# Attention's value products: two key tiles together, one pair behind the scores

## The chip, the cores and the metric

The kernel runs on one core of a Trainium2 chip. The metric is the device time of one execution in microseconds (us), the median of several runs. The core's engines are TensorE (in the profile PE for the matrix products and PEld for the loads of their weights), VectorE (DVE), ScalarE (ACT), GpSimd (POOL) and SyncE (SP), which here issues the loads and stores. Each engine works through its own instructions in order, and semaphores make one wait for another.

## What is computed

Two blocks of a small sequence model, on 1024 tokens of 1024 features (and 16 prefixed tokens in the first block, 256 context tokens in the second). The change touches the attention in the last mixer of the second block: 8 heads, 1024 queries, 1280 keys (1024 of the sequence, 256 of the context), keys and queries of 96 features, values of 64.

```python
def _block_attention(q, k, v):
    ...
    scale = dk ** -0.5
    def one(qi):
        s = jnp.einsum('bqhd,bkhd->bhqk', qi, k, preferred_element_type=jnp.float32) * scale
        p = jax.nn.softmax(s, axis=-1).astype(v.dtype)
        return jnp.einsum('bhqk,bkhd->bqhd', p, v)
    ...
```

The attention's result is gated and goes with the other half of the mixer into a closing product and a layer norm (`_cd_out`, `_post_norm`).

## The kernel before

The program is one long unrolled list of instructions. The writer of the kernel calls engines in some order; a scheduler then orders each engine's instructions by their priority (the order in which they were written, unless told otherwise) and by a model of when their inputs are ready, gives out buffers of the pools, and sets the semaphores. So a line's place in the code is not its place on the engine.

Most matrix products multiply numbers split into two parts of a shorter format (float32r), in three products instead of one. The stages before the attention (first block, context path, Fourier mixer) take the first 2770 us of the profile. Then:

`prep(h)` makes ready head h's keys (L1500 to L1505: 6 products, copies on ScalarE, sums and splits on VectorE) and queries (L1508 to L1524: two blocks of 6 products L1516, a rotation and a split that go back and forth between ScalarE and VectorE). Then it takes the maximum of the scores from their leading parts: 24 products L1531 into the PSUM pool `psm` (4 banks, tag `sm`), each followed by a reduction on VectorE (L1532); the maxima are negated (L1536), transposed (L1538), and put as a row 96 into the queries through DRAM (L1540 to L1542), so that the score products subtract them.

`attend(h)` goes over the 1280 keys in KT = 10 tiles of 128. For a tile t and each half c of the queries (512 of them), three products L1555 make the scores in a bank of `pmm` (4 banks, tag `mm`), and ScalarE takes their exponential into `P` (L1556; 4 such tiles in the pool). Two products L1558 add the tile's share to the values' sum `po` (a bank of `psm`): the half c goes into the output partitions 64c to 64c + 63, so each uses 64 of the 128 columns of TensorE's array. They are in full float32, and each shows as two records in the trace. The softmax's sums are made by adding up the P tiles, even and odd ones in `sa0` and `sa1` (L1561, L1563; odd tiles of heads 0 to 5 on GpSimd, but for the last, the others on VectorE), and by four more products with ones behind the loop, L1573, the closing sums below: sa0 and sa1, for each half of the queries. Then come a reciprocal (L1575), the gate (L1569, L1576) and copies (L1582).

While head h is attended, `prep(h + 2)` runs beside it for h up to 5: the generator `nxt` is moved on by one step after each tile. Heads 6 and 7 have no such company; there the first inputs of the closing product are loaded and split (`split_in`, L74 to L76).

Of the kernel before, what the change touches and what calls it, by code (L numbers as in the profile page):

```python
# [11 lines left out]
AF = mybir.ActivationFunctionType  # L12
# [25 lines left out]
class Build:  # L38
# [20 lines left out]
    # ---- weights: raw -> exact split into two float32r parts  # L59
# [8 lines left out]
    # the sources side by side into the two parts of t  # L68
# [9 lines left out]
    # X: function (part, k, lo, hi) -> AP ; W: tile [128, 2, nk*128]  # L78
# [18 lines left out]
    # rsqrt(ps * scale + eps), one Newton step on top of the table's value  # L97
# [30 lines left out]
    # exp(x) in place on a small tile, x clamped to [-87, 88]  # L128
# [26 lines left out]
    # sin(th + shift) with the range brought to [-pi, pi]; shift 0 or pi/2  # L155
    def exact_sin(self, pool, out, th, shape, shift):
# [7 lines left out]
        if shift:  # L164
            # rounding of the sum above drops the quarter; redo it in two steps
            v.tensor_scalar(out=n, in0=th, scalar1=I2P, scalar2=0.25, op0=ALU.mult, op1=ALU.add)
            v.tensor_scalar(out=n, in0=n, scalar1=M, scalar2=None, op0=ALU.add)
# [14 lines left out]
    # ================= block 1 =================  # L182
# [20 lines left out]
    def block1(self, upto):  # L203
# [32 lines left out]
        # panel 1 (queries), 2 (values) of a head; 0: gates  # L236
# [13 lines left out]
    def z_panel(self, pool, tag, bufs=None):  # L250
        """the next product of the normed input that is wanted later only, kept in DRAM: queries and
        values of heads, tanh(x / 2) of the merge gates"""
# [17 lines left out]
    # panels chunk by chunk, where the chunks of X come one after the other  # L270
# [7 lines left out]
    def s5_params(self, pool, w1):  # L278
# [37 lines left out]
        # powers a^0..a^8, ascending (pa) and descending (pd)  # L316
# [18 lines left out]
        # bb = coef * b  # L335
# [10 lines left out]
        # scan multipliers [Ar|Ar], [-Ai|Ai]  # L346
# [7 lines left out]
    def cmul_tab(self, pool, pw, r0, r1, co, i):  # L354
        """out[128, 2, 4, 8, 16] = pw (over t) * co (over h) for the four pairs of panel i"""
# [15 lines left out]
    def s5(self):  # L371
# [5 lines left out]
        with ExitStack() as es:  # L377
# [17 lines left out]
            # first panels token chunk by token chunk, under the norm of the next chunk  # L395
# [3 lines left out]
            for c, (lo, hi) in enumerate(CH1):  # L399
                pss = [self.ps_mm()[:, 0:hi - lo] for _ in ws]  # L400
                # as the inputs of the first chunk come
# [19 lines left out]
            for i in range(8):  # L421
# [9 lines left out]
                # maps  # L431
# [28 lines left out]
                # chunk inputs to the states  # L460
# [7 lines left out]
            # outputs' factors, real and imaginary states on top of each other  # L468
# [6 lines left out]
            # scan over the chunks  # L475
# [9 lines left out]
            # outputs  # L485
            for i in range(8):
# [7 lines left out]
                # re(a^t c) over -im(a^t c)  # L494
# [24 lines left out]
    # ---- hgrn2  # L519
    def hgrn(self):  # L520
        nc, tc, A = self.nc, self.tc, self.A
        v = nc.vector
        with ExitStack() as es:
# [39 lines left out]
            for hd in range(8):  # L563
                # projections
# [28 lines left out]
                # decays inside the chunks of 16  # L593
# [16 lines left out]
                # queries and keys against the middle of their chunk of 32; QI: block, key chunk, query  # L610
# [3 lines left out]
                # meta chunk  # L614
# [8 lines left out]
                # chunk totals  # L623
# [9 lines left out]
                # queries decayed from the start of their chunk of 32, then from the middles of earlier chunks  # L633
# [7 lines left out]
                # products over the chunks of 16 before and after in the block of 128  # L641
# [14 lines left out]
                # queries against the carried state (in place of R)  # L656
                tt(out=R.rearrange("p (a s) -> p a s", s=32), in0=Qs.rearrange("p (a s) -> p a s", s=32), in1=pe2[:, :, 0].unsqueeze(2).to_broadcast([128, 32, 32]), op=ALU.mult)
                # keys into the state (in place of Bx)
                tt(out=B4[:, :, 0], in0=k4[:, :, 0], in1=B16(sx2, 0), op=ALU.mult)
                tt(out=B4[:, :, 1], in0=B4[:, :, 1], in1=B16(sx2, 1), op=ALU.mult)  # L660
                # token-major values and keys
# [16 lines left out]
                # states before each block  # L678
# [12 lines left out]
                # outputs  # L691
# [19 lines left out]
                # norm over the head's features, gate  # L711
                # (four token ranges side by side in the columns of the array, brought back by selections)
# [23 lines left out]
    # exact split of an fp32 tile into the two parts of t[:, :, lo:hi]  # L736
# [13 lines left out]
    # a product whose result goes on to a norm: the first panels panel by panel, the last nres  # L750
    # panels token chunk by token chunk, so that the norm of a chunk runs under the next chunk.
    # sq: the norm needs the sum of squares (else the plain sum) over all panels' rows r(i, lo, hi);
    # done(c, lo, hi, ps) gets that sum in every partition
# [43 lines left out]
    # sum over partitions of ns sources of n columns, in every partition: four sources at a time side  # L797
    # by side in the columns of the array, their sums brought together by a last product; the last
    # tail sources go into that one directly. tmp(): an [128, >= n] tile
# [22 lines left out]
    def merge(self):  # L822
# [5 lines left out]
        with ExitStack() as es:  # L828
# [50 lines left out]
            # h1 = h + (2 m) @ w_out / 2, then its norm  # L879
# [3 lines left out]
            # in place of the product's input, which a finished chunk no longer needs  # L883
# [109 lines left out]
    # ================= block 2 =================  # L993
    def mods(self, pool, cp):
        """shift, 1 + scale, gate / ALPHA of c (column 0) and c_ctx (column 1), features on partitions;
        the weights stream past the conditions, 128 inputs to 1024 features at a time"""
# [37 lines left out]
    # layer norm over features of a token chunk of x + gate / ALPHA * y, which is ALPHA * x + gate * y  # L1034
    # but for the scale: eps / ALPHA ** 2. r(k): AP of feature tile k, ps: its sum over features;
    # emit(k, d, rs): centred rows and 1 / deviation
    # sqt(k): tile for the squares of row k
# [15 lines left out]
    # LN(x) and the next mixer's input: n * g + b, n * g (1 + scale) + b (1 + scale) + shift  # L1053
# [16 lines left out]
    def ab_mixer(self, tp, yp, X, T, chunks, half_out, fill):  # L1070
        """pool heads then gating heads; half_out(which, tiles) takes the four feature tiles"""
# [86 lines left out]
    def ctx_path(self):  # L1158
        """the context through the first mixer and to the keys of the second"""
# [73 lines left out]
    # latent and rotary key rows of the second mixer, into DRAM at token base  # L1233
# [126 lines left out]
    def fourier(self, cp, tp, X):  # L1360
# [9 lines left out]
        # tokens on partitions, later in their place the spectra  # L1370
# [28 lines left out]
        # latents  # L1399
# [10 lines left out]
        # transform over tokens, then over features  # L1410
# [31 lines left out]
    def latents(self, tp, cq):  # L1442
        """normed latents, key weights"""
# [21 lines left out]
        # keys: both parts of the weights side by side in the columns  # L1465
# [7 lines left out]
    def mla(self, X):  # L1473
# [9 lines left out]
        with ExitStack() as es:  # L1483
            c0 = es.enter_context(self.pool("ml", side="right"))
            # key buffers: rows 0-63 the head's, 64-95 rotary, 96 ones against the row of -max
# [8 lines left out]
            def prep(h, tp):  # L1494
# [31 lines left out]
                # maximum of the scores, from their leading parts  # L1526
# [17 lines left out]
            def attend(h, nxt, tp):  # L1544
                """scores (keys on partitions), softmax weights, values"""
# [3 lines left out]
                P = {}  # L1549
                for t in range(KT):  # L1550
                    Pt = P[t] = tp.tile([128, 2, 512], F32, tag="P", name=self.nm("P"), bufs=4)
                    for c in range(2):
                        ps = self.ps_mm()
                        for i, (kp, qp) in enumerate(((0, 0), (0, 1), (1, 0))):
                            nc.tensor.matmul(ps, K[0:97, kp, 128 * t:128 * t + 128], Q[0:97, qp, 512 * c:512 * c + 512], start=i == 0, stop=i == 2)  # L1555
                        nc.scalar.activation(Pt[:, c], ps, AF.Exp, scale=scale)  # L1556
                    for c in range(2):
                        nc.tensor.matmul(po[64 * c:64 * c + 64, :], vv(t)[:, 64 * h:64 * h + 64], Pt[:, c], start=t == 0, stop=t == KT - 1)  # L1558
# [3 lines left out]
                    elif t > 3:  # L1562
                        eng.tensor_tensor(out=sa[t % 2], in0=sa[t % 2], in1=Pt, op=ALU.add)  # L1563
# [249 lines left out]
```

## Time and profile before

| | us |
|---|---|
| median of 3 runs | 3249.68 |
| lowest, highest run | 3247.68, 3250.23 |
| profiled execution: its span, first to last instruction | 3242.6 |
| of it, attention with the preparation of its first heads | 2770.0 to 3105.5 |
| before that | 0 to 2770.0 |
| closing product, layer norm | 3105.5 to 3242.6 |

For the profiled execution only the span is given, not a time taken from outside; it is 7.1 us below the median. All names of lines, L1558 and the like, are those of the kernel before; behind the change the lines of `attend` stand lower, and the sections that show its rows say which is which.

### The profile page before, as it was taken

The page shows a single profiled execution, that of the slowest core. Times are in us where ns is not written, and L with a number is a line of the kernel's source. Part 1 is how long each engine was busy: PE and PEld are TensorE (multiplying, and loading weights), DVE is VectorE, ACT ScalarE, POOL GpSimd, SP SyncE. Part 2 cuts the span into 40 slices and gives each one's busy share as a digit, 9 for nine tenths or more (in the row PEclk, how much of TensorE's full clock was granted, in tenths as well). Part 3 has the DMA queues.
Part 4 walks back from the last instruction along what each step waited for, and adds up shares of the span by engine and source line. Part 5 has one row for each costly group of instructions (what it writes and reads, how often), then busy time and mean ns, then how long its engine had stood idle before and what let it go on. Part 6 is the DMA issues. An engine that isn't in the chain of part 4 may idle for free.

```text
span 3242.6 us, 47786 instructions
## 1 busy us (share of the span) xinstructions
PE 3165.4 (98%) x19986; PEld 2840.8 (88%) x19986; DVE 1831.4 (56%) x3508; ACT 1126.1 (35%) x1846; POOL 92.9 (3%) x99
## 2 busy tenths in 40 slices
PE   8999899999999999999999999999999999999998
PEld 6999887879999999999999999989997889555476
DVE  7549468775454334465554555455336464777744
ACT  5341733233344312232222222252224353544532
POOL 0000000000210000000000000000000000121100
PEclk9999999999999999999999999999999999999999
DMA  4342454343552234111111111111111223000211
GB/s 153 90 161 91 148 182 142 118 153 103 158 155 81 91 118 130 33 59 46 40 46 53 47 52 40 53 35 54 46 40 66 92 88 130 29 7 7 79 49 52
DMA packets 106384, 269.01 MB, mean 83 GB/s; under 512 B 14798, under 2 KB 43694, under 8 KB 105974
## 3 DMA queue, kind: packets, MB, share of 16 engines
q1 hardware_dynamic: 99656, 245.35, 23.3%
q10 hardware_dynamic: 4464, 16.34, 1.3%
q0 software_dynamic: 2048, 4.26, 0.7%
q8 instruction: 157, 2.57, 0.3%
q14 instruction: 59, 0.48, 0.0%
HBM read 219.12 MB, written 46.11 MB: 82 GB/s over the span
## 4 chain that ended last, share of the span: by engine, by line
PE 90%; DVE 4%; DMA 2%; ACT 2%; issue 1%; SPq 0%; DVEq 0%; ACTq 0%
PE mm L83 62%; PE mm L949 7%; PE sm L1558 4%; PE mm L1555 4%; PE sm L813 2%; PE mm L1124 2%; PE sm L1531 1%; DMA YBd<-o 1%; PE mm L1516 1%; ACT Tt L502 1%; DVE R L604 1%; PE sm L465 1%; PE sm L1573 0%; PE sm L708 0%; PE sm L1017 0%
## 5 line engine op out<-in xcount | busy, mean ns | idle before, releaser
L83 PE MATMUL mm<-z,whl 128*128 128x256 f32 (+3 forms) x4032 | 682.9, 325 | 1.5 <-ACT z L231 1.0
L83 PE MATMUL mm<-a,whl 128*128 128x384 f32 (+1 forms) x4320 | 682.7, 319 | 1.6 <-ACT u L917 1.6
L83 PEld LDWEIGHTS mm<-a,whl 128*128 128x128 f32 x4320 | 678.5, 188 | 3.7 <-ACT u L917 1.9
L83 PEld LDWEIGHTS mm<-z,whl 128*128 128x128 f32 x4032 | 637.6, 189 | 36.8 <-issue 29.2
L76 DVE TENSOR_TENSOR whl<-wraw,whl 128x1024 fp32r<-128x1024 f32 (+2 forms) x258 | 302.6, 1178 | 221.1 <-ACT whl L75 220.3
L75 ACT CAST whl<-wraw 128x1024 fp32r<-128x1024 f32 (+2 forms) x258 | 260.6, 1014 | 341.8 <-PE mm L949 137.0
L83 PE MATMUL mm<-hx,whl 128*128 128x384 f32 (+1 forms) x2232 | 366.3, 322 | 7.7 <-ACT fx L1378 7.1
L83 PEld LDWEIGHTS mm<-hx,whl 128*128 128x128 f32 x2232 | 352.0, 189 | 16.8 <-ACT fx L1378 7.3
L949 PE MATMUL mm<-g,whl 128*128 128x384 f32 (+1 forms) x1584 | 257.9, 322 | 2.3 <-DVE f L951 1.2
L949 PEld LDWEIGHTS mm<-g,whl 128*128 128x128 f32 x1584 | 248.0, 188 | 13.9 <-issue 8.1
L83 PE MATMUL mm<-b,whl 128*128 128x384 f32 (+1 forms) x1152 | 180.9, 319 | 0.0
L83 PEld LDWEIGHTS mm<-b,whl 128*128 128x128 f32 x1152 | 180.8, 189 | 0.0
L917 ACT COPY u<-mm 128x384 f32<-128x384 f32 x132 | 58.3, 445 | 317.8 <-PE mm L83 317.8
L951 DVE TENSOR_TENSOR f<-f,mm 128x384 f32<-128x384 f32 (+1 forms) x240 | 118.3, 508 | 71.3 <-PE mm L949 70.4
L1556 ACT ACTIVATE P<-mm 128x512 f32<-128x512 f32 x160 | 94.7, 597 | 134.4 <-PE mm L1555 127.9
L83 PEld LDWEIGHTS mm<-y,whl 128*128 128x128 f32 x816 | 120.2, 188 | 13.1 <-issue 9.8
L83 PE MATMUL mm<-y,whl 128*128 128x256 f32 (+1 forms) x816 | 128.1, 312 | 1.4 <-ACT y L741 1.1
L1558 PE MATMUL sm<-P,m 128*64 128x512 f32 x320 | 128.0, 611 | 0.6 <-ACT P L1556 0.5
L1532 DVE TENSOR_REDUCE mx<-sm 128x1 f32<-128x512 f32 (+1 forms) x192 | 105.7, 595 | 39.7 <-PE sm L1531 38.4
L1555 PE MATMUL mm<-m,KB 97*128 97x512 f32 x420 | 121.7, 405 | 0.0
L1555 PEld LDWEIGHTS mm<-m,KB 97*128 97x128 f32 x420 | 75.6, 188 | 47.4 <-issue 33.3
L923 DVE TENSOR_SCALAR av<-u,conv_w,conv_b 128x1024 f32<-128x1024 f32 x22 | 17.9, 812 | 138.7 <-ACT u L917 138.7
(519 smaller groups left out, 3664.0 us busy)
## 6 DMA issues: line engine op xcount, KB each, us to landing
wraw<-w_up SPq DMA_DIRECT2D x44, 512.0 KB, 3.2
wraw<-w_h SPq DMA_DIRECT2D x32, 512.0 KB, 3.4
wraw<-ab_w SPq DMA_DIRECT2D x32, 512.0 KB, 3.4
wm<-ab_w_mod SPq DMA_DIRECT2D x24, 512.0 KB
wm<-cd_w_mod SPq DMA_DIRECT2D x24, 512.0 KB, 4.0
wraw<-w_down SPq DMA_DIRECT2D x22, 512.0 KB, 3.2
ut<-Ud SPq DMA_DIRECT2D x16, 520.0 KB, 4.5
gt<-Gd SPq DMA_DIRECT2D x16, 513.0 KB, 3.2
```

The lines of the kernel that those rows point to most:

```text
L75: self.nc.scalar.copy(t[:, 0], raw)
L76: self.nc.vector.tensor_tensor(out=t[:, 1], in0=raw, in1=t[:, 0].bitcast(F32), op=ALU.subtract)
L83: nc.tensor.matmul(ps, W[:, wp, wofs + 128 * k:wofs + 128 * k + 128], X(xp, kofs + k, lo, hi), start=first and k == 0 and i == 0, stop=las ...
L813: nc.tensor.matmul(p4[32 * j:32 * j + 32], self.ones[:, 0:32], x, start=i < 4, stop=i - len(pend) + j + 5 >= m)
L917: return u, (self.split_w(A["w_up"][p], [1024]), lambda c, lo, hi, ps: nc.scalar.copy(u[:, lo:hi], ps))
L949: nc.tensor.matmul(ps, ws[j][:, wp, 128 * o:128 * o + 128], G[j][:, xp, lo:hi], start=n_ == 0 and i == 0, stop=n_ == len(js) - 1 and i == 2)
L951: v.tensor_tensor(out=h1[o][:, 2 + lo:2 + hi], in0=h1[o][:, 2 + lo:2 + hi], in1=ps, op=ALU.add)
L1124: nc.tensor.matmul(ps, X(xp, k, 128 * t, 128 * t + 128), wv[k // 4][:, wp, 256 * (k % 4):256 * (k % 4) + 256], start=k == 0 and i == 0, st ...
L1532: v.tensor_reduce(out=mx[:, qt, j:j + 1], in_=ps, axis=mybir.AxisListType.X, op=ALU.max)
L1555: nc.tensor.matmul(ps, K[0:97, kp, 128 * t:128 * t + 128], Q[0:97, qp, 512 * c:512 * c + 512], start=i == 0, stop=i == 2)
L1556: nc.scalar.activation(Pt[:, c], ps, AF.Exp, scale=scale)
L1558: nc.tensor.matmul(po[64 * c:64 * c + 64, :], vv(t)[:, 64 * h:64 * h + 64], Pt[:, c], start=t == 0, stop=t == KT - 1)
```

## The change

`attend` no longer issues a tile's two value products right behind its exponentials. A function `values` issues the four of two tiles (t, c) = (a, 0), (a, 1), (b, 0), (b, 1); it is called after an odd tile for the two tiles of the pair before, and once behind the loop for the last pair. The products are written under a raised priority, and the first of the four gets an edge to the last exponential of the pair's second tile: the edge orders the scheduler and sets no semaphore (`NoSync`). The two calls that add up the P tiles stay where they were. Elsewhere the diff only takes comments out.

```diff
                 P = {}
+                def values(ts):
+
+                    with self.tc.high_priority():
+                        for t in ts:
+                            for c in range(2):
+                                mm = nc.tensor.matmul(po[64 * c:64 * c + 64, :], vv(t)[:, 64 * h:64 * h + 64], P[t][:, c], start=t == 0, stop=t == KT - 1)
+                                if t == ts[0] and c == 0:
+                                    self.tc.add_manual_dep(mm.ins, E[ts[1]].ins.name, mybir.DependencyInfo(
+                                        mybir.DependencyClass.NoSync, mybir.DependencyReason.DATA), reason="pair")
+
+                E = {}
+
                 for t in range(KT):
                     Pt = P[t] = tp.tile([128, 2, 512], F32, tag="P", name=self.nm("P"), bufs=4)
                     for c in range(2):
                         ps = self.ps_mm()
                         for i, (kp, qp) in enumerate(((0, 0), (0, 1), (1, 0))):
                             nc.tensor.matmul(ps, K[0:97, kp, 128 * t:128 * t + 128], Q[0:97, qp, 512 * c:512 * c + 512], start=i == 0, stop=i == 2)
-                        nc.scalar.activation(Pt[:, c], ps, AF.Exp, scale=scale)
-                    for c in range(2):
-                        nc.tensor.matmul(po[64 * c:64 * c + 64, :], vv(t)[:, 64 * h:64 * h + 64], Pt[:, c], start=t == 0, stop=t == KT - 1)
+                        E[t] = nc.scalar.activation(Pt[:, c], ps, AF.Exp, scale=scale)
...
                         eng.tensor_tensor(out=sa[t % 2], in0=sa[t % 2], in1=Pt, op=ALU.add)
+                    if t % 2 and t > 1:
+                        values((t - 3, t - 2))
                     next(nxt, None)
+                values((KT - 2, KT - 1))
```

How the rows move on TensorE is shown at three places. In the rows, mm and sm are banks of the two PSUM pools, P the exponentials, m_25199 to m_25201 the values of all heads, KB a head's keys, whl and cqn the query weights and their inputs, ones and sa the closing sums. Behind the change the value products are L1555 (before: L1558), the score products L1567 (before: L1555) and the closing sums L1586 (before: L1573).

First place: TensorE in head 1, from the values of tile 2 to the query products behind those of tile 3, beside the preparation of head 3's queries. Before:

```order
L1558 MATMUL sm_25687<-P_25732,m_25199 64x512 x2
L1500 MATMUL mm_25746<-ckn,wk 128x256 x2
L1555 MATMUL mm_25755<-m_25236,KB_25195 128x512 x3
L1555 MATMUL mm_25760<-m_25236,KB_25195 128x512 x3
L1516 MATMUL mm_25770<-cqn_23878,whl_24900 128x512
L1558 MATMUL sm_25687<-P_25754,m_25199 64x512 x2
L1516 MATMUL mm_25770<-cqn_23878,whl_24900 128x512 x2
L1516 MATMUL mm_25770<-cqn_23879,whl_24900 128x512 x3
```

With the change:

```order
L1567 MATMUL mm_25749<-m_25236,KB_25195 128x512 x3
L1567 MATMUL mm_25754<-m_25236,KB_25195 128x512 x3
L1516 MATMUL mm_25766<-cqn_23878,whl_24900 128x512
L1555 MATMUL sm_25687<-P_25728,m_25199 64x512 x2
L1555 MATMUL sm_25687<-P_25748,m_25199 64x512 x2
L1516 MATMUL mm_25766<-cqn_23878,whl_24900 128x512 x2
L1516 MATMUL mm_25766<-cqn_23879,whl_24900 128x512 x3
```

Tile 2's products, which stood ahead of tile 3's scores, have come down to stand in front of tile 3's; the place of the pair is the place that tile 3's had, one matmul behind its scores.

Second place: TensorE later in the same head, tiles 8 and 9 (P_25911 and P_25943 before, P_25907 and P_25937 with the change), among the products for the maxima of head 3. Before:

```order
L1558 MATMUL sm_25687<-P_25911,m_25201 64x512
L1555 MATMUL mm_25944<-m_25236,KB_25195 128x512
L1531 MATMUL sm_25902<-KB_24401,m_25768 128x512
L1555 MATMUL mm_25944<-m_25236,KB_25195 128x512 x2
L1555 MATMUL mm_25949<-m_25236,KB_25195 128x512 x3
L1555 MATMUL mm_25983<-m_25475,KB_25196 128x512
L1531 MATMUL sm_25905<-KB_24401,m_25768 128x512
L1558 MATMUL sm_25687<-P_25943,m_25201 64x512
L1531 MATMUL sm_25908<-KB_24401,m_25768 128x256
L1531 MATMUL sm_25925<-KB_24401,m_25768 128x512
L1558 MATMUL sm_25687<-P_25943,m_25201 64x512
```

With the change:

```order
L1567 MATMUL mm_25943<-m_25236,KB_25195 128x512 x2
L1531 MATMUL sm_25898<-KB_24401,m_25764 128x512
L1555 MATMUL sm_25687<-P_25907,m_25201 64x512 x2
L1555 MATMUL sm_25687<-P_25937,m_25201 64x512 x2
L1531 MATMUL sm_25901<-KB_24401,m_25764 128x512
L1531 MATMUL sm_25904<-KB_24401,m_25764 128x256
L1531 MATMUL sm_25919<-KB_24401,m_25764 128x512
L1567 MATMUL mm_25983<-m_25471,KB_25196 128x512 x3
```

The rows before begin with the second half of tile 8. The maxima's products that stood between the two halves of a tile now stand behind the pair, three in a row.

Third place: TensorE at the change from head 1 to head 2. Before:

```order
L1538 MATMUL sm_25959<-ident_99,nmx_25957 8x128
L1573 MATMUL sm_25969<-sa_25688,ones 64x512 x2
L1573 MATMUL sm_25969<-sa_25689,ones 64x512 x2
L1558 MATMUL sm_25979<-P_25982,m_25199 64x512 x2
L1558 MATMUL sm_25979<-P_26003,m_25199 64x512 x2
L1555 MATMUL mm_26030<-m_25475,KB_25196 128x512
```

With the change:

```order
L1538 MATMUL sm_25955<-ident_99,nmx_25953 8x128
L1586 MATMUL sm_25969<-sa_25688,ones 64x512
L1555 MATMUL sm_25979<-P_25982,m_25199 64x512 x2
L1555 MATMUL sm_25979<-P_26001,m_25199 64x512 x2
L1586 MATMUL sm_25969<-sa_25688,ones 64x512
L1586 MATMUL sm_25969<-sa_25689,ones 64x512 x2
L1500 MATMUL mm_26032<-ckn,wk 128x256 x2
```

The first pair of head 2 has moved in behind the first of head 1's four closing sums.

## Rows read from the trace of the kernel before

**Rows 1.** The page's first part: span, busy time by engine.

```profile
span 3242.6 us, 47786 instructions
...
PE 3165.4 (98%) x19986; PEld 2840.8 (88%) x19986; DVE 1831.4 (56%) x3508; ACT 1126.1 (35%) x1846; POOL 92.9 (3%) x99
```

**Rows 2.** Windows: stretch, length; busy time (instructions) by engine; clock, DMA share, GB/s.

```profile
2792.40:2830.70 38.30, 37.84 (x137) 18.90 (x138) 28.06 (x44) 17.77 (x33) 6.42 (x4) 1.00 0.00 1
2830.70:3047.20 216.50, 215.40 (x761) 110.94 (x759) 163.45 (x225) 102.25 (x178) 41.46 (x19) 1.00 0.04 12
2919.60:2962.00 42.40, 42.40 (x155) 22.08 (x153) 32.47 (x46) 19.84 (x35) 7.74 (x3) 1.00 0.02 7
3047.20:3105.50 58.30, 58.30 (x190) 24.23 (x186) 34.12 (x28) 33.49 (x49) 0.00 (x0) 1.00 0.36 126
```

**Rows 3.** The page's costliest groups: line, engine, operation, count; busy us, mean ns; idle.

```profile
L1558 PE MATMUL sm<-P,m 128*64 128x512 f32 x320 | 128.0, 611 | 0.6 <-ACT P L1556 0.5
```

**Rows 4.** Timeline of TensorE, blocks of value products: start, length, records.

```profile
2877.90 1.83 PE L1558 MATMUL sm<-P,m 128*64 128x512 f32 x4
...
2891.18 1.07 PE L1558 MATMUL sm<-P,m 128*64 128x512 f32 x2
...
3047.24 3.60 PE L1558 MATMUL sm<-P,m 128*64 128x512 f32 x16
...
3056.65 1.08 PE L1558 MATMUL sm<-P,m 128*64 128x512 f32 x4
```

**Rows 5.** Timeline of TensorE, 2880.0 to 2886.1 us, head 2.

```profile
2880.00 1.57 PE L1555 MATMUL mm<-m,KB 97*128 97x512 f32 x6
2881.40 0.40 PE L1516 MATMUL mm<-cqn,whl 128*128 128x512 f32 x1
2881.74 1.59 PE L1558 MATMUL sm<-P,m 128*64 128x512 f32 x4
2883.26 1.42 PE L1516 MATMUL mm<-cqn,whl 128*128 128x512 f32 x5
2884.51 1.56 PE L1555 MATMUL mm<-m,KB 97*128 97x512 f32 x6
```

**Rows 6.** Timeline, weight loads and ScalarE there; brackets: idle before, its releaser.

```profile
2881.73 0.19 PEld L1558 LDWEIGHTS sm<-P,m 128*64 128x64 f32 x2 [0.37 <-ACT P L1556]
2882.25 0.19 PEld L1558 LDWEIGHTS sm<-P,m 128*64 128x64 f32 x2 [0.33 <-ACT P L1556]
...
2880.90 1.30 ACT L1556 ACTIVATE P<-mm 128x512 f32<-128x512 f32 x2 [0.33 <-PE mm L1555]
```

**Rows 7.** Timeline of TensorE, the end of head 7.

```profile
3101.96 1.07 PE L1573 MATMUL sm<-sa,ones 128*64 128x512 f32 x2
3102.87 1.84 PE L1558 MATMUL sm<-P,m 128*64 128x512 f32 x4
```

**Rows 8.** Timeline of VectorE behind the closing sums, change from head 2 to 3.

```profile
2920.14 3.35 DVE L1575 RECIPROCAL rz<-sm 128x512 f32<-128x512 f32 x1
...
2923.96 0.67 DVE L1576 TENSOR_TENSOR gt<-gt,rz 128x512 f32<-128x512 f32 x1
...
2925.15 0.41 DVE L1503 TENSOR_TENSOR kt<-kt,mm 64x256 f32<-64x256 f32 x1
2926.57 1.19 DVE L1505 TENSOR_TENSOR KB<-kt,KB 64x256 fp32r<-64x256 f32 x1 [1.01 <-ACT KB L1504]
2927.79 0.69 DVE L1520 TENSOR_TENSOR qu<-mm,ropet 64x512 f32<-64x512 f32 x1
2929.11 1.23 DVE L1563 TENSOR_TENSOR sa<-sa,P 128x1024 f32<-128x1024 f32 x1 [0.63 <-ACT P L1556]
2930.37 0.68 DVE L1522 TENSOR_TENSOR qt<-qt,qu 32x512 f32<-32x512 f32 x1
```

**Rows 9.** Waits in heads 0 to 7, and reductions' busy time in head 2919.6:2962.0.

```profile
PEld sm L1531 <- DVE mx L1532: 16.1, 19, 1.4
...
2919.60:2962.00 42.40, 13.31 (x24) 1.00 0.02 7
```

## The prediction

> **What bounds the kernel now.** I read the page's first part first [rows 1]: TensorE is busy for 98% of the span and its granted clock is 1.00 in every window below, so time can only go where TensorE's own stream gets shorter, or come where it stops. Next I read the windows of the attention stage [rows 2]: head 0, heads 1 to 5, one of those alone, heads 6 and 7. TensorE is busy practically all the time in each, while VectorE has 163.45 of 216.50 us in heads 1 to 5 and ScalarE 102.25. A busy TensorE is not a full one, though, and the third view shows it: the products of the values (L1558) alone take 128.0 us, for 160 products in 320 records (two records make one product) [rows 3].
>
> The timeline tells why that is dear. One product standing alone, a block of 2 records, takes 1.07 us [rows 4]. Where both query halves of a tile are ready, the block of 4 records takes 1.08 us: the halves write different 64 output columns and go side by side, so the second costs nothing. But mostly a tile's block of 4 takes 1.59 or 1.83 us [rows 4, 5]. The weight loads say what for: the second half's load at 2882.25 ends a wait of 0.33 us for ScalarE's exponential [rows 6]. Two exponentials take 1.30 us in a row, from 2880.90 to 2882.20 [rows 6], and the score products that feed the later one had ended about 2881.4: the values stand directly behind their own scores, so half c=0 starts and half c=1 comes 0.52 to 0.76 us later. Eight halves that need not wait (16 records, 4 tiles) take 3.60 us [rows 4], that is 0.43 us more for each half-step of both columns: (3.60 - 1.08) / 6 = 0.42.
>
> Counted through the timeline from 2792.4 to 3104.5, start to start (which leaves out the 0.07 us by which a block's last record overlaps the next one), the 80 tiles stand in 91 blocks: 48 single products of 1.00 (24 tiles), 14 blocks of 1.76, 16 of about 1.52, 4 of 1.02, 9 blocks joined to others or to the closing sums (22 tiles, 19.8 us). Together 120.9 us; 128.0 less 91 tails of 0.08 gives the same.
>
> **The change, part by part.** *Values in pairs.* In the new order all four products of two tiles stand together, in all 40 pairs. A pair alone takes one tile's 1.01 and two further steps of 0.43: 1.87 us. 29 pairs stand alone, 54.2 us; 11 stand next to another pair or to the closing sums, where four steps of 0.43 suffice, 19.1 us. Sum 73.3 instead of 120.9: **48 us less**. The exponentials should be there: between the last score product of the pair's second tile and the pair there are one to three matmuls, and the first tile's two steps take another 0.9 us, so the half that waited until 0.85 us behind its scores (2881.4 to 2882.25) is asked for only 1.2 us behind them.
>
> *Fewer changes of kind.* Entering a block of values costs TensorE something besides: the L1516 matmul before the block takes 0.34 us to the block's start, where six L1555 take 1.40, 0.233 each; the five behind it take 1.25 to 2884.51 instead of 1.17 [rows 5]. I take 0.19 a block. 91 blocks become 38 (4 in head 0, 5 in each of heads 1 to 5 and 7, 4 in head 6): 53 x 0.19 = **10 us less**.
>
> *The closing sums.* Before, the four sums of a head (L1573) stand together, and 8 records take 1.94 us, after which the next head's values follow. Now, at six changes of head, the first pair of the next head has slipped in behind the first sum. That sum holds column half 0; the first value product wants the same half and stands ahead of the one for half 1. In the one place of the trace with this order, the sum's two records start at 3101.96 and the value product of half 0 only at 3102.87 [rows 7]; half 1 starts later still, but it also waited for its exponential, so the row leaves open whether it would have gone ahead. Either four steps of 0.86 remain (0) or there are five (0.86 a head). I take the dear end, since nothing in the trace starts ahead of an earlier product that waits: 6 x 0.86 = **5 us more**. The Trainium skill, TensorE: Matmul & The Clock Gate, Part 3: Packing small matmuls, says that matmuls start in program order; by it the 5 us stand, without it they would be 0.
>
> TensorE's sum: 48 + 10 - 5 = 53 us less. By head: 6 in head 0, 3.6 in head 6, 8 in head 7, which leaves about 35 for heads 1 to 5, or 43.3 to 36 us a head.
>
> *What is late next.* VectorE is busy 32.47 us in a head of 42.40 [rows 2]; in one of 36 it has 3.5 to spare. Two places can fail. First, the chain behind the closing sums. The reciprocal (3.35) starts when they end; behind it come the gate product (0.67, its step 0.6), the last key piece (0.41 and 1.19), the query rotation (0.69 and 0.68) [rows 8], between them three ScalarE steps of about 0.6 and two exponentials ahead of the last of them. Before the head's first maximum product (L1531) can start, that is about 3.3 + 0.4 + 0.6 + 1.2 + 0.7 + 0.6 + 0.7, and 1.8 for the exponentials and the copy: 9.3 us. In the new order TensorE has between the same two points two short matmuls, 30 of 0.234, and one pair with its entry: 0.24 + 7.0 + 2.06 = 9.3. So the cover is just used up. Second, the maxima: three products now come in a burst behind each pair, with three score banks to take them, and the reductions that free these banks already kept weight loads waiting 19 times, 16.1 us, most of it covered [rows 9]. This new cost is not in the trace; it lies between 0 (cover holds) and the 4 to 5 us a head at which VectorE would keep half of its present idle time. I take 1 us a head for six heads, nearer to 0 because VectorE's own work of the maxima part, 24 reductions in 13.3 us [rows 9] and two additions of 1.23, fits into the 19 us that TensorE has there, and 2 us at the very end, where the last pair has no later scores to cover its exponential and the last addition (1.23). **8 us more.**
>
> *At nothing* I cost: ScalarE (some 20 of 36 us a head), GpSimd's additions (7.74 us a head, far from the end), the loads for the closing product (the DMA engines are 36% busy in the last window, [rows 2]; if they came late, the time lost would be theirs, a few us at most), and the held P tiles: there are four, the pair reads the older two before the next tile's scores are done.
>
> Sum: 53 - 8 = 45 us. The profile's span is 3242.6 us, 7.1 under the median of the runs, 3249.7; the rest lies around the span and isn't touched. So 3249.7 - 45 = **3205 us**.
>
> **The rivals.** *All of it.* If the sums don't cost a fifth step and VectorE stays covered, 58 - 1 = 57 us go: 3193. For it: VectorE has 3.5 us a head over. Against: the chain that just fits.
>
> *VectorE sets the pace.* It then keeps its present waits of 8 to 9 us a head beside its 32.47, some 41 us a head: heads 1 to 5 give 216.5 - 205 = 11.5, the others 15.6: 27 us, **3223**. For it: reductions and products hang on three banks, and today's weight loads already wait for them. Against: those waits are mostly for TensorE itself. The Trainium skill, TensorEngine Tiling (Array Packing), PSUM Bottleneck, warns of just this: side-by-side products speed up TensorE but not the reading of PSUM, which may become the bottleneck. No trace here shows it yet.
>
> *Nothing side by side.* If the second half's delay were not the exponential but something fixed, blocks would take 1.5 to 1.8 a tile as now and only the 10 us for changes remain, less the 5: 3245, within what I call the same. The block of 1.08 and the 3.60 for four tiles [rows 4] speak against it.
>
> *Slower.* ScalarE takes its work in order, and in the new order its copies that wait for VectorE (the gate, the rotated queries) stand ahead of tile 4's exponentials, which the third pair needs. If the 9.3 us chain stood uncovered in front of that pair at each of six heads, 6 x 9.3 = 56 us would be added to a gain of 53, with 5 to 10 for what queues behind: 3255 to 3260. It decides from 8.8 us a head. Against it: thirty matmuls and a pair cover it.
>
> **How the numbers follow.** Forecast 0.60, all of it 0.15, VectorE's pace 0.17, nothing side by side 0.04, slower 0.04. The first three are faster by more than 0.2% (6.5 us, about what a measurement of this kernel can tell from no change): 0.92; same 0.04; slower 0.04. The forecast's own range is 3198 to 3215 (5 us for the sums, 10 for VectorE); with the neighbours on both sides, 3191 to 3225.
>
> **What would show it.** The values' busy time should fall from 128.0 to about 76 us, in blocks of 8 records of 1.94; weight loads of values waiting for the exponential should nearly vanish; heads 1 to 5 should last 36 to 38 us, with VectorE near 90% and its waits for maximum products shorter; the closing sum's records should show one step of half 0 alone. Blocks of 8 that still take 3 us, or heads of 41 us with weight loads waiting for reductions, would prove me wrong.

## The result and the profile after

The changed kernel takes 3194.30 us (median of 4 runs, 3191.73 to 3194.65), the kernel before beside it 3248.68 (4 runs, 3244.17 to 3250.23): a ratio of 0.9839, 95% interval 0.9825 to 0.9852, or 54.4 us less. The forecast was 3205 with a range of 3191 to 3225: right in sign and inside the range, 11 us too careful.

Behind the change the value products are L1555, the scores L1567, the exponentials L1568, the additions of the P tiles L1571 and L1573, the closing sums L1586, the reciprocal L1588 and the gate products L1582 and L1589. The preparation keeps its lines.

The page's first part answers to [rows 1]: VectorE and ScalarE do what they did, TensorE is busy 56 us less.

```profile
span 3192.9 us, 47786 instructions
PE 3109.1 (97%) x19986; PEld 2838.8 (89%) x19986; DVE 1830.5 (57%) x3508; ACT 1121.4 (35%) x1846; POOL 93.1 (3%) x99
```

The windows answer to [rows 2]. They run from one L1538 to the next, which is where the preparation of a head ends: head 0, head 1, heads 2 to 5, one of those alone, heads 6 and 7. Columns as there.

```profile
2794.12:2824.13 30.01, 29.12 (x126) 17.52 (x125) 26.72 (x42) 15.62 (x29) 5.48 (x3) 1.00 0.00 1
2824.13:2864.99 40.86, 37.92 (x155) 22.99 (x154) 34.70 (x46) 19.98 (x37) 11.02 (x6) 0.96 0.03 7
2864.99:3008.23 143.24, 142.16 (x607) 86.06 (x606) 128.41 (x181) 80.17 (x145) 31.64 (x14) 1.00 0.05 16
2936.37:2972.10 35.73, 35.42 (x152) 21.39 (x151) 31.83 (x46) 19.28 (x36) 7.48 (x3) 1.00 0.02 8
3008.23:3056.62 48.39, 47.81 (x202) 24.84 (x201) 35.74 (x30) 32.67 (x52) 0.00 (x0) 1.00 0.43 152
```

A steady head went from 42.40 to 35.73 us, with TensorE still busy all but 0.3 of it and VectorE now at 31.83 of 35.73, 89%. One head stands out: head 1, 40.86 us, with 2.9 us in which TensorE does nothing and a mean granted clock of 0.96. Between the same instructions of the kernel before, head 0 took 36.50, heads 1 to 5 216.56 and heads 6 and 7 (to the last closing sum) 62.1; now 30.01, 184.10 and 48.39. That is 52.7 us less. Of it the span shows 49.7, since the stages ahead of the attention took 1.9 and those behind it 1.1 us longer in this execution.

TensorE's timeline at the change from head 3 to head 4 and behind it answers to [rows 4, 5, 7]. Records of two lines that overlap are listed apart.

```profile
2936.37 0.28 PE L1538 MATMUL sm<-ident,nmx 128*8 128x128 f32 x1
2936.57 0.64 PE L1586 MATMUL sm<-sa,ones 128*64 128x512 f32 x1
2936.59 0.64 PE L1555 MATMUL sm<-P,m 128*64 128x512 f32 x1
2937.05 0.59 PE L1586 MATMUL sm<-sa,ones 128*64 128x512 f32 x1
2937.07 1.87 PE L1555 MATMUL sm<-P,m 128*64 128x512 f32 x6
2938.40 0.59 PE L1586 MATMUL sm<-sa,ones 128*64 128x512 f32 x1
2938.77 0.59 PE L1555 MATMUL sm<-P,m 128*64 128x512 f32 x1
2938.82 1.45 PE L1586 MATMUL sm<-sa,ones 128*64 128x512 f32 x5
2940.21 0.50 PE L1500 MATMUL mm<-ckn,wk 128*128 128x256 f32 x2
...
2942.27 1.94 PE L1555 MATMUL sm<-P,m 128*64 128x512 f32 x8
2944.14 1.42 PE L1516 MATMUL mm<-cqn,whl 128*128 128x512 f32 x5
```

The pair at 2942.27 is as forecast: 8 records in 1.94 us, 1.87 to the next start; all 29 lone pairs of the attention are like it. The place above it was forecast wrongly. In program order the first closing sum, for half 0, is followed by the pair's products for half 0, half 1, half 0, half 1, and then by the other sums. The first sum (2936.57) holds column half 0; the first value product wants that half too and must wait. Yet a value product starts 0.02 us behind the sum (2936.59), so it can only be the next in order, the one for half 1. From 2936.57 to 2940.21 the four sums and the pair take 3.64 us: four steps, not five.

Three of the waits from 2794 to 3057 us (us in total, times, longest):

```profile
PEld sm L1531 <- DVE mx L1532: 15.1, 24, 2.4
PEld sm L1555 <- ACT P L1568: 8.0, 28, 0.3
PE sm L1531 <- DVE mx L1532: 3.3, 5, 1.9
```

The value products' loads waited 31.7 us in 79 places for exponentials before, now 8.0 in 28, none over 0.3. The loads of the maxima wait for reductions much as they did [rows 9].

### The profile page after: what moved, and what is told of

It reads as the page before. It is cut to its first block, busy times and chain, and to the rows that moved or that the text cites. A ratio compares the mean times of both kernels' runs of the same rounds, so it can differ in the third digit from the quotient of the medians.

```text
span 3192.9 us, 47786 instructions
## 1 busy us (share of the span) xinstructions
PE 3109.1 (97%) x19986; PEld 2838.8 (89%) x19986; DVE 1830.5 (57%) x3508; ACT 1121.4 (35%) x1846; POOL 93.1 (3%) x99
## 4 chain that ended last, share of the span: by engine, by line
PE 87%; DVE 6%; ACT 3%; DMA 3%; issue 1%; SPq 0%; DVEq 0%; ACTq 0%
PE mm L83 63%; PE mm L949 7%; PE mm L1567 3%; PE sm L813 2%; PE sm L1555 2%; PE mm L1124 2%; DMA YBd<-o 1%; PE sm L1531 1%; ACT Tt L502 1%; DVE R L604 1%; PE sm L465 1%; DMA wm<-ab_w_mod 0%; PE sm L708 0%; PE sm L1017 0%; PE sm L687 0%
## 5 line engine op out<-in xcount | busy, mean ns | idle before, releaser
L1567 PE MATMUL mm<-m,KB 97*128 97x512 f32 x420 | 118.2, 401 | 1.3 <-ACT P L1568 1.3
L1568 ACT ACTIVATE P<-mm 128x512 f32<-128x512 f32 x160 | 91.5, 596 | 68.6 <-PE mm L1567 50.9
L1567 PEld LDWEIGHTS mm<-m,KB 97*128 97x128 f32 x420 | 76.9, 191 | 24.9 <-issue 7.3
L923 DVE TENSOR_SCALAR ag<-u,conv_w,conv_b 128x1024 f32<-128x1024 f32 x22 | 17.9, 813 | 119.1 <-ACT u L917 119.1
```

Source lines behind the costliest of these rows:

```text
L1568: E[t] = nc.scalar.activation(Pt[:, c], ps, AF.Exp, scale=scale)
```

## The experiments

Times of runs are medians; each ratio is against the kernel before on the same chip, and the changed kernel's is 0.9839. The stages ahead end at 2764 us in one profiled execution and at 2770 in another, so I also compare "the attention", from the start of the first L1538 to the start of the last record of the closing sums: 343.6 us before, 291.0 changed. "Blocks" are TensorE's unbroken stretches of value products and closing sums, from a block's start to the start of what follows: 92 with 137.0 us before, 38 with 88.5 changed.

**e_onecol: nothing side by side.**

```diff
-mm = nc.tensor.matmul(po[64 * c:64 * c + 64, :], vv(t)..., P[t][:, c], start=t == 0, stop=t == KT - 1)
+o = po[64 * c:64 * c + 64, :] if t == 0 else po[0:64, :]
+mm = nc.tensor.matmul(o, vv(t)..., P[t][:, c], start=t == 0, stop=c == 1 if t == 0 else t == KT - 1 and c == 1)
```

> The changed kernel, where the values' products of half 1 go into the output partitions of half 0 from the second tile on, so that no two of them can go side by side: the sums of the values of both halves run together and the attention's output is another; count and size of the instructions stay. Theory (side by side is what makes the second half free): 0.86 us more for each of 9 tiles in 8 heads, 62 us: 3256, a lone pair 3.6 us instead of 1.87. Rival (products of the two halves do not overlap much; the gain came from waits and fewer blocks): 3194 to 3215.

Measured: 3255.69 us, ratio 1.0030 (1.0019 to 1.0041). A lone pair:

```profile
2884.55 3.65 PE L1556 MATMUL sm<-P,m 128*64 128x512 f32 x8
2888.13 1.44 PE L1516 MATMUL mm<-cqn,whl 128*128 128x512 f32 x5
```

3.58 us to the next start instead of 1.87; blocks 149.8 us, 61 more than changed, and the time 61 more. The theory's 62 stands: the column halves are worth more than the whole gain.

**e_single and e_behind: one tile at a time.** In e_single `values((t - 1,))` is called after each tile (and for the last one behind the loop), with the edge to that tile's own last exponential, `E[ts[-1]]`.

```diff
-if t % 2 and t > 1:
-    values((t - 3, t - 2))
+if t:
+    values((t - 1,))
```

> The changed kernel, but with the values of one key tile at a time, one tile behind the scores, under the same priority and edge. TensorE's order then has 66 blocks of value products and closing sums, 55 of them one tile standing alone, where the changed kernel has 38 (29 lone pairs) and the kernel before 92. Theory (what pays is that both query halves of a tile are ready and go side by side; an entry into a block costs about 0.19 us): 55 lone tiles at 1.01 us and 25 joined ones at 0.86 give 77 us instead of 73, and 28 more entries cost 5: about 9 us more than the changed kernel's 3194, so 3203. Rival (what pays is the number of blocks: 54 us for 54 blocks, 1 us each): 28 us more, 3222.

Measured: 3226.66 us, 0.9942 (0.9929 to 0.9954). By number that is the rival, but the trace says why it didn't test it. The edge put each block right behind its own exponential, so the second half was late again, as before the change (the row is for 2794 to 3060 us; to the end of the attention it is 28.9 us in 77 waits):

```profile
PEld sm L1555 <- ACT P L1568: 25.2, 66, 0.9
```

```profile
2923.70 1.90 PE L1555 MATMUL sm<-P,m 128*64 128x512 f32 x4
2925.53 1.44 PE L1567 MATMUL mm<-m,KB 97*128 97x512 f32 x5
```

I had moved two things at once. The 55 lone tiles took 1.49 us on average, not 1.01. Against e_single, e_behind moves the edge alone, to the next tile's exponential (the diff is against the changed kernel; the calls are those of e_single):

```diff
-... E[ts[1]].ins.name, ...
+... E[min(t + 1, KT - 1)].ins.name, ...
```

> The changed kernel with one tile's value products at a time, each block put behind the last exponential of the next tile, so that both its halves have long been ready. (In the run e_single the block stood right behind its own tile's exponentials, and its loads still waited for them 66 times, 25.2 us; it did not tell the entries' price.) TensorE's order has 64 blocks, 47 of them one lone tile, instead of 38 with 29 lone pairs. Theory (waiting for the exponential was the cost; an entry costs 0.19): lone blocks of 1.01, together 76 us instead of 73, 26 entries more at 0.19 cost 5: 8 us more than the changed kernel, 3202, and the loads' wait for exponentials stays near nothing. Rival (it is the number of blocks that costs, 1 us each, as e_single's 32 us for 28 blocks would also have it): 26 us more, 3220.

Measured: 3199.40 us, 0.9855 (0.9838 to 0.9871).

```profile
2904.76 1.08 PE L1555 MATMUL sm<-P,m 128*64 128x512 f32 x4
2905.77 1.43 PE L1516 MATMUL mm<-cqn,whl 128*128 128x512 f32 x5
```

All 47 lone tiles take 1.01, the wait for exponentials is 2.3 us, and 64 blocks cost hardly more than 38: 36.47 us a steady head instead of 35.73. Of these 0.74 the blocks' own steps make 0.45, which leaves 0.1 for each of three more entries. So one tile at a time, with both halves ready, already has some nine tenths of the gain (28 of the 54 blocks fewer are part of that); pairing brings the rest.

**e_noedge: priority alone.** The three lines of the edge are taken out.

> The changed kernel without the edge, the raised priority kept. TensorE's order falls apart again: 90 blocks, 49 of them a single half of a tile, as good as the 92 with 48 single halves of the kernel before. Theory (only the order counts, and the edge makes it): 3240 to 3250, the single halves 1.00 us each. Rival (the priority brings the values forward and with that most of the gain): below 3215.

Measured: 3244.33 us, 0.9989 (0.9980 to 0.9998); blocks 131.8 us, 49 single halves of 1.00, loads waiting 25.9 us for exponentials in the attention (before: 31.7). As expected, the edge makes the order; priority without it brings 4 us.

**e_crossed: how far a product may overtake.**

```diff
-for t in ts:
-    for c in range(2):
+for c in range(2):
+    for t in ts:
```

> The changed kernel with each pair's four products in another order: tile a half 0, tile b half 0, tile a half 1, tile b half 1. Nothing else moves. Theory (each half of the columns has a queue of its own, so a product for a free half starts ahead of an earlier one that waits for the other half, as the closing sums of the changed kernel show): no change, 3194 within 3, blocks of 8 records of 1.94. Rival (matmuls start in program order, as the prediction took it for the closing sums): in each pair the second half-0 product holds up half 1 by 0.86 us; 40 pairs, 34 us, 3228.

Measured: 3202.94 us, 0.9871 (0.9855 to 0.9886): neither number, and the trace shows both theories at work in different places. The change from head 3 to head 4 and the first lone pair behind it:

```profile
2939.81 1.07 PE L1586 MATMUL sm<-sa,ones 128*64 128x512 f32 x2
2940.72 1.94 PE L1555 MATMUL sm<-P,m 128*64 128x512 f32 x8
2942.43 1.94 PE L1586 MATMUL sm<-sa,ones 128*64 128x512 f32 x6
2944.30 0.50 PE L1500 MATMUL mm<-ckn,wk 128*128 128x256 f32 x2
...
2946.36 1.94 PE L1555 MATMUL sm<-P,m 128*64 128x512 f32 x8
```

In the lone pair a half-1 product stands behind one waiting half-0 product and overtakes it: 1.87 us, as in 21 of the 29 lone pairs. In seven others half 1 began 0.13 to 0.48 us behind half 0, and one ran at a granted clock of 0.67 (1.99 to 2.77 us). At the change of head it stands behind two waiting ones and does not: the sum runs alone for 0.91 us and the block takes 4.49 instead of 3.64. Five such places and one of 6.21 instead of 5.35 make 5.2 us, the eight slower pairs 2.8; the attention is 7.2 us longer.

**e_quad4: groups of four.**

```diff
-if t % 2 and t > 1:
-    values((t - 3, t - 2))
+if t in (3, 7):
+    values(range(t - 3, t + 1))
...
-... E[ts[1]].ins.name, ...
+... E[ts[-1]].ins.name, ...
```

> The changed kernel with groups of four, four and two tiles instead of five pairs, still with four P tiles: 29 blocks of values and closing sums instead of 38. Theory (TensorE sets the time; a lone block costs 0.15 us beyond its steps of 0.43 and 0.19 for the entry): 9 blocks fewer, 3 us less: 3191. Rival (ScalarE: the exponentials of the fifth tile can't start until the group has read the first, and nothing feeds VectorE for 3.6 us, which at 90% cannot catch up): 1 to 2 us more a head, 3200 to 3210.

Measured: 3200.91 us, 0.9860 (0.9846 to 0.9875). By number this is the rival: 37.2 us a steady head, 1.5 more. TensorE stops there for 1.6 us a head, the longest stop just ahead of the second group (the bracket: idle before, its releaser):

```profile
2918.73 0.50 PE L1531 MATMUL sm<-KB,m 96*128 96x512 f32 x1 [1.19 <-DVE mx L1532]
2919.51 3.65 PE L1555 MATMUL sm<-P,m 128*64 128x512 f32 x16
```

TensorE waits there for VectorE's reductions, not for ScalarE's exponentials. But what made VectorE late just ahead of the stop is an addition on GpSimd, the matter of the next runs:

```profile
2915.85 2.10 DVE L1522 TENSOR_TENSOR qt<-qt,qu 32x512 f32<-32x512 f32 x1
```

```profile
2915.01 2.39 POOL L1573 TENSOR_TENSOR sa<-sa,P 128x1024 f32<-128x1024 f32 x1 [7.71 <-ACT P L1568]
```

L1522 takes 0.68 us where no addition runs. Here it ended 0.55 us behind GpSimd's, and the reduction behind it came 1.4 us late; heads 1 to 5 each have such an L1522 (2.10 to 2.11 us) and a stop of 1.19 to 1.20 behind it. So most of the loss lies behind a collision; that longer bursts of maxima alone would cost anything is not shown, since groups of four with GpSimd's additions elsewhere were not run.

**e_swap, e_swap2: GpSimd's additions out of VectorE's way.** Head 1 of the changed kernel, VectorE and GpSimd, then TensorE:

```profile
2831.35 1.16 DVE L1571 TENSOR_TENSOR sa<-P,P 128x1024 f32<-128x1024 f32 x1
2832.43 2.89 DVE L1589 TENSOR_TENSOR gt<-gt,rz 128x512 f32<-128x512 f32 x1
...
2841.39 2.38 DVE L1524 TENSOR_TENSOR m<-qt,m 96x512 fp32r<-96x512 f32 x1 [0.32 <-ACT m L1523]
2843.81 0.68 DVE L1522 TENSOR_TENSOR qt<-qt,qu 32x512 f32<-32x512 f32 x1
2844.52 1.29 DVE L1532 TENSOR_REDUCE mx<-sm 128x1 f32<-128x512 f32 x2
```

```profile
2831.27 3.50 POOL L1571 TENSOR_TENSOR sa<-P,P 128x1024 f32<-128x1024 f32 x1 [18.08 <-ACT P L1568]
...
2840.86 2.37 POOL L1573 TENSOR_TENSOR sa<-sa,P 128x1024 f32<-128x1024 f32 x1 [4.20 <-ACT P L1568]
```

```profile
2845.27 0.50 PE L1531 MATMUL sm<-KB,m 96*128 96x512 f32 x1 [1.93 <-DVE mx L1532]
...
2846.48 1.48 PE L1567 MATMUL mm<-m,KB 97*128 97x512 f32 x3
```

L1524 takes 0.69 elsewhere; here it ends 0.54 us behind GpSimd's addition. The first reduction comes behind it, TensorE waits 1.93 us for the bank that it frees, and afterwards three score products take 1.48 us instead of 0.86. The four windows, before the stop, in it, and two behind it, show the granted clock in the eighth column (instruction counts in brackets not counted): 1.00, 1.00, 0.60 (partly at the lower level, 1.2 GHz), and 1.00 again.

```profile
2838.00:2843.20 5.20, 5.13 (x21) 2.75 (x21) 4.58 (x5) 3.90 (x8) 2.34 (x1) 1.00 0.17 48
2843.20:2845.30 2.10, 0.17 (x2) 0.03 (x1) 2.04 (x4) 0.77 (x2) 0.03 (x1) 1.00 0.00 0
2845.30:2849.60 4.30, 4.30 (x12) 3.14 (x12) 4.12 (x7) 1.65 (x4) 0.00 (x0) 0.60 0.00 0
2849.60:2853.00 3.40, 3.40 (x16) 1.70 (x16) 1.75 (x4) 0.48 (x1) 2.36 (x1) 1.00 0.02 5
```

The same work is moved, nothing is taken away (e_swap has `t in (3, 6, 7)`):

```diff
-eng = nc.gpsimd if t % 2 and t < KT - 1 and h < 6 else v
+eng = nc.gpsimd if t in (6, 7, 8) and h < 6 else v
```

> The changed kernel, with one addition of the P tiles exchanged between VectorE and GpSimd in heads 0 to 5: tile 5's goes to VectorE, tile 6's to GpSimd; the work of both stays the same. It takes GpSimd's addition away from the place where the changed kernel's head 1 lost about 5 us (40.9 us against 35.7 in heads 2 to 5): there VectorE's L1524 lasted 2.38 us instead of 0.69 while GpSimd added, ScalarE and then TensorE waited (1.9 us), and TensorE's granted clock was 0.5 for the next 3.5 us. Theory (VectorE operations with both sources in SBUF wait while GpSimd adds, and that stall started the rest): head 1 lasts 36 to 37 us, 3190 to 3191. Rival (VectorE is simply full in head 1; where GpSimd adds does not matter): tile 5's addition puts 1.2 us ahead of the first maxima of each head; no change to 6 us more, 3194 to 3200.

Measured: 3191.48 us, 0.9832 (0.9818 to 0.9845); head 1 38.06 us. L1524 is back at 0.68, stop and slow clock are gone; the first collision (L1589, 2.89 us) is left, and so are three score products more than heads 2 to 4 have; 2.8 us came back instead of 4 to 5.

> The changed kernel with GpSimd's three additions of a head moved to tiles 6, 7 and 8 (heads 0 to 5), where VectorE mostly reads maxima from PSUM; VectorE takes tiles 3 and 5. In e_swap, which moved one of them, head 1 went from 40.9 to 38.1 us, L1524 from 2.38 back to 0.69, and TensorE's 1.9 us stall with the half clock behind it was gone; what was left there was L1589 at 2.89 us beside GpSimd's first addition, and 1.0 us of TensorE waiting behind it. Theory (VectorE's operations with two SBUF sources wait for GpSimd's addition): L1589 falls to 0.67, head 1 to 36.5 to 37 us, the attention is 1 us shorter than e_swap, 4 to 5 shorter than the changed kernel: 3190. Rival (the 1.2 us added ahead of the first maxima lengthens the chain that only just is covered): 0.2 to 1.2 us more in each of heads 1 to 5: 3192 to 3198.

Measured: 3188.77 us, 0.9821 (0.9806 to 0.9836). The repeat, with the changed kernel beside it on one chip:

> The changed kernel once more, beside the next run on the same chip: 3194, the attention 291 us from the first L1538 to the last closing sum, head 1 at 40.9 us with TensorE's stall of 1.9 us, if that stall belongs to the kernel and not to one execution.

> The run e_swap2 once more (GpSimd's additions at tiles 6, 7 and 8), beside the changed kernel on the same chip. Theory (6.4 us of the attention went with GpSimd's additions out of VectorE's way, 291.0 to 284.6): 5 to 7 us under the changed kernel's median. Rival (the difference was that of two executions): the same median within 2 us.

Measured: 3193.50 against 3188.67 us, ratios 0.9839 (0.9824 to 0.9854) and 0.9820 (0.9806 to 0.9835). The intervals overlap, so the 4.8 us alone would not settle it; the attention does: 291.0 and 290.9 us in both executions of the changed kernel, 284.6 and 284.7 in both of the other. Head 1 of the changed kernel takes 40.88 us again in r_after, with a stop of 1.94 us, so the stop belongs to the kernel. In r_swap2 (VectorE's L1589, then the windows of heads 1 and 2):

```profile
2830.63 0.67 DVE L1589 TENSOR_TENSOR gt<-gt,rz 128x512 f32<-128x512 f32 x1
```

```profile
2822.79:2858.17 35.38, 35.33 (x153) 21.65 (x152) 30.94 (x46) 19.81 (x37) 8.04 (x4) 1.00 0.03 8
2858.17:2894.82 36.65, 36.00 (x152) 21.52 (x151) 32.97 (x46) 19.57 (x36) 8.46 (x4) 1.00 0.03 8
```

Head 1 is as short as any now. Head 2 still has one L1524 of 2.91 us beside an addition of GpSimd, and it is the longest. This is the best version found.

**e_dve, b_dve: all additions on VectorE.** `eng = v` in the changed kernel and in the kernel before.

> The changed kernel with all additions of the P tiles on VectorE, none on GpSimd: three more of 1.22 us a head for heads 0 to 5, two of them ahead of the first maxima. Theory (VectorE has room: 31.8 us of 35.7, of which 1.6 were waiting beside GpSimd, so 33.9 of 35.7 now; the stall of head 1 goes): heads 2 to 5 at 35.7 to 36.5, head 1 at 36 to 37, 3190 to 3195. Rival (VectorE, the only reader of the maxima, already sets the pace at 90%): 2 to 3.7 us more a head, 3205 to 3215.

Measured: 3196.79 us, 0.9845 (0.9830 to 0.9859).

```profile
2900.66:2936.75 36.09, 35.30 (x151) 21.84 (x152) 34.03 (x49) 19.30 (x36) 0.00 (x0) 1.00 0.03 8
```

Heads 1 to 5 all take 36.1 to 36.3: no collision, no long head 1, and 0.5 us a steady head for VectorE at 94%. VectorE has room, but little; the time is 2 us above the range expected, since head 0 and the end also grew by 1.3 and 1.6.

> The kernel before with all additions of the P tiles on VectorE, none on GpSimd: 32.47 us of VectorE's work in a head of 42.4 become about 34. Theory (TensorE sets the time and the waits beside GpSimd were covered, but for part of the 2.6 and 1.5 us by which heads 1 and 2 are longer than the others): no change to 4 us less, 3244 to 3249. Rival (VectorE's chain before the maxima is on the path already): 1 us or more a head longer, 3255.

Measured: 3256.74 us, 1.0028 (1.0017 to 1.0038). A miss: 44.3 us a steady head instead of 42.4.

```profile
2921.33:2965.55 44.22, 43.44 (x151) 21.98 (x151) 34.09 (x49) 19.56 (x36) 0.00 (x0) 1.00 0.03 6
```

TensorE idles 0.8 us of the 1.8 that this head is longer. With other engines' times the scheduler also orders TensorE anew: 64 single halves of a tile instead of 48, 139.7 us of blocks instead of 137.0. In this head the blocks are 0.7 us longer and TensorE's work outside them 0.3. The rival's number came, but more than half of it by TensorE's own longer work, which neither theory named.

## Why the prediction was right, and where it was off

*Values in pairs, 48 us less:* right. The value products, start to start, took 120.9 us before and 74.2 now (73.3 forecast), 46.7 less. e_onecol shows that it is the halves side by side, e_behind that it takes both exponentials to be there. L1555's busy time is 82.1, not 76, because at the changes of head its records interleave with the closing sums and the profile counts the stretch for both.

*Fewer changes of kind, 10 us:* right for the change as a whole. Outside its blocks TensorE had 25.38 us of a steady head before and 24.31 now (idle time left out), with 6 entries fewer: 0.18 each, 54 of them 9.7 us. In e_behind an entry came to only 0.1, so it is not one fixed price.

*The closing sums, 5 us more:* wrong. The step that failed is "I take the dear end, since nothing in the trace starts ahead of an earlier product that waits". The price is 0: sums 16.1 us before, 14.3 now. The row it rested on [rows 7] left the question open, as the text said, because half 1 also waited for its exponential there. The Trainium skill, TensorE: Matmul & The Clock Gate, Part 3: Packing small matmuls, has matmuls start in the order of the program; the rows at 2936.57 and 2936.59 above differ, and decide.

*VectorE, 8 us more:* near in size, but not by the mechanism forecast, so that the size came out is luck. "1 us a head for six heads" was nearly nothing in heads 2 to 5 (35.7 us, TensorE idle 0.2 to 0.34), where the cover of 9.3 us did just hold: in two of them the first maximum product waits 0.17 us for ScalarE's cast of the queries. Nor did the end cost 2 us: heads 6 and 7 gained 13.7 where 11.6 less those 2 were forecast. What was lost was lost in head 1, 40.86 us against 35.7: 2.6 us more of idle time, some 1.7 by the lower clock (4.3 us at 0.60), and most of the rest for three score products more than heads 2 to 4 have (155 matrix products against 152 in the windows). The step that failed here is the term "at nothing" for GpSimd's additions. In place of a late chain there was a collision of VectorE and GpSimd that I had not read in the trace of before, although L1505's 1.19 us for 64x256 in [rows 8] (0.42 where no addition ran) pointed at it: GpSimd added from 2924.68 to 2927.48 there, and L1505 ended 0.28 us later.

Over the whole attention the blocks got 48.5 us shorter and TensorE's work outside them 8.1 (9.8 but for the clock in head 1), while its idle time grew by 3.9: 52.7 us less. The forecast had 45: 43 for values and sums, 10 for entries, less 8. The medians differ by 54.4 because the profiled execution of before was one of its shorter ones: in the later runs a run's time lies 1.9 us above its span (3192.96 and 3191.1 in r_after), not 7.1, so that it came to some 3244.5.

Of the rivals, "all of it" (3193) was nearest in number: one of its two conditions, no fifth step, held, the other, VectorE covered throughout, failed in head 1. "VectorE sets the pace" is not what happened at 89%, and at 94%, in e_dve, it cost 0.5 us of 36; no run here shows where it begins to. "Nothing side by side" and "slower" are excluded by e_onecol and by heads of 35.7 us (the sum for "slower", 56 against 53 with 5 to 10 more, makes 3258 to 3263, not 3255 to 3260).

## What to carry to other kernels

Products that use half of the columns are only free beside each other if both inputs are ready when the first is asked for: put them behind the next step's scores, not behind their own exponential, and hold the order with an explicit edge, since priority alone left 49 halves standing alone. When one engine's stream gets shorter, look for operations of the now nearly full engine that last longer than their kind elsewhere, and see what runs beside them. An edge that moves a block changes both its company and what it waits for; test the two apart, as e_behind does and e_single did not.

## What the runs showed of the hardware that was not expected

Products for different column halves can start out of program order: one overtook one waiting product of the other half (0.02 us behind the sum, 2936.57 and 2936.59), and in e_crossed none overtook two (0.91 us alone at 2939.81). So on TensorE's two column halves the order of starts is not that of the program. How far the look ahead reaches in other arrangements was not tried.

When VectorE had an operation with both sources in SBUF while GpSimd added two tiles, one of the two waited. Where VectorE did, L1524 took 2.38 and 2.91 us instead of 0.69, and L1589 2.89 instead of 0.67. Where GpSimd did, its addition took 3.50 instead of 2.37, although VectorE's L1571 began 0.08 us behind it. Reductions, which read PSUM, kept their 0.69 us beside it. The collisions were there before the change (L1524 at 2936.14 took 1.70 us) and are in heads 2 to 5 of the changed kernel (L1589 1.59 to 1.67 us, L1522 1.21 to 1.23 instead of 0.68); there they are covered. The Trainium skill, SBUF — State Buffer, SBUF: two separate sides, tells of a pair of ports shared by the two, which one of them holds for a whole instruction; the trace agrees: 3.50 us are the 2.37 of the addition and some 1.16 of VectorE's L1571, and L1524 ended 0.54 us behind GpSimd's.

After TensorE had stood for 1.9 us, its granted clock fell to 0.60 on average over the next 4.3 us. In r_swap2's heads 1 and 2, which have no such stop, it stayed at 1.00.
